# A two-layer hybrid transformer trunk on one core: weight pieces in other buffers, and each engine's order set by a list scheduler inside the kernel

## The chip, the core and the metric

The kernel runs on one core of a Trainium2 chip. The core has five instruction streams that matter here: TensorE (PE, matrix products; PEld is its weight load), VectorE (DVE), ScalarE (ACT), GpSimd (POOL) and SyncE (SP), which issues every DMA of this kernel. Each stream runs its instructions in the order in which they stand in the program; between streams, semaphores say when a result may be used. The metric is the device time of one execution in microseconds (us); lower is better.

## The reference

The input x is 512 tokens by 1024 features, all float32. Two layers, each with a mixing half and a feed-forward half, then a last norm:

```python
mod = jax.nn.silu(c) @ ada_w + ada_b            # six vectors of 1024
h = rms_norm(x, norm_mix) * (1 + sc_m) + sh_m
(aq, ak, av, bq, bkc, bvc, bks, bvs, bkw, bvw, bg, cqkv, cz, ca, cb) = jnp.split(h @ w_in, points, axis=-1)
o_a = banded_attention(rope(aq), rope(ak), av, window=128, sinks)        # 4 heads, 128-token band
o_b = nsa_mixer(bq, bkc, bvc, bks, bvs, bkw, bvw, bg, ...)               # compressed + selected + window
o_c = gated_delta_net(cqkv, ca, cb, cz, conv_w, A_log, dt_bias, norm_w)  # chunked delta rule, 4 heads of 128
x = x + gt_m * (jnp.concatenate([o_a, o_b, o_c], axis=-1) @ w_out)
h = rms_norm(x, norm_ffn) * (1 + sc_f) + sh_f
gate, up = jnp.split(h @ w_gate_up, 2, axis=-1)
x = x + gt_f * ((jax.nn.silu(gate) * up) @ w_down)
```

Inside `nsa_mixer`, `compress_tokens` maps overlapping blocks of 32 tokens through a two-layer network (`silu(flat @ w1) @ w2`), for keys and for values; `w1` is 2048 by 256 for each. Inside `gated_delta_net`, a unit lower triangular matrix per chunk and head is inverted, and a state of 128 by 128 per head is carried from chunk to chunk.

## The kernel before

All activations are kept transposed (features on partitions, 512 tokens along the free axis). A product with a weight is done as three matmuls on float32r: each weight tile `wraw` from DMA is split into a high part `whi` (ACT copies it, L584) and a low part `wlo` (DVE subtracts, L585; sometimes POOL), and `product` multiplies high by high, high by low and low by high. A full-width product of this kind takes 24 matmuls of 128x512.

The mixing half (`layer`) runs, in the order in which it is written: the values of all branches (`pvt`); the delta rule's projections with their short convolutions (`pj`, `convs`); its decays and chunk matrices (`pgr`, `pbr`, `pkk`); the inversion of the chunk matrices, which is a series of small products `pi` on TensorE with a copy by DVE or ACT after each (`prio("inv")`), begun by a substitution on POOL in the tile `lane`; the walk over four chunks (`prio("chain")`: `pks`, `pvn`, `pqs`, `psu`, `pin`, and `pot` for the output); the projections for the two attention branches (`single`, `pair`, with `rope`); the compression (`squeeze`, four pieces of `w1`, products `pcmp`); the attention itself (`attend`: scores `psc`, the mask and row maximum on DVE, exp on ACT, scaling on DVE and POOL, transposes `ppt`, values `poa`, `pob`); and the product with `w_out` in two parts (`pwc` for the delta rule's rows, `pw` for the attention's). The feed-forward half runs over six groups of columns (`pg`, `pu`, then `pd`; from the fifth tile of layer 1 with a seven-product scheme, `pm`). During layer 0 a side stream (`ada`) computes modulation vectors from `ada_w` through the tiles `araw`, on ACT, POOL and DVE.

Weights come through a ring of two buffers, tag `wraw` in pool `wr`, 1 MB each. Each DMA into it waits on SP until the split of the tile two places before is done, and every later DMA stands behind it in SP's queue. The four compression pieces (`craw`, 1 MB each) pass through the same ring, as do the keys of the banded branch (`AK`, 512 KB). Three buffers of 512 KB, tags `ab0` to `ab2`, hold `aq`, `bq` and `bqr` from their projection on; in layer 0 before that the side stream's `araw2` takes turns in them.

What sets the order: the instructions are recorded as the program is written, and the tile framework then orders each engine's stream by its own simulated timeline, shifted by priorities that the kernel gives (`prio`, from the tables `BASE` and `KS`, one table per half layer).

## Time and profile before

| | |
|---|---|
| median of 3 runs | 1449.24 us (1446.93 to 1449.49) |
| profiled execution, its own time | 1450.83 us |
| its span, first to last instruction | 1449.1 us |
| mean granted TensorE clock | 0.968 of full |
| PE, DVE, ACT, POOL busy | 1363.4, 975.1, 685.9, 496.9 us |

The span is 1.7 us short of the execution's own time. Busy time of PE is the union of its matmuls' spans, whose ends are modelled; a gap in it is a stretch in which no matmul was under way. The granted clock is given for each stretch as a mean over time: TensorE ran either at full speed (2.4 GHz) or at half (1.2 GHz), so a mean of 0.83 over a stretch says that it had half the clock in 34% of it.

### The profile page before, as it was taken

The page shows a single profiled execution, that of the slowest core. Times are in us where ns is not written, and L with a number is a line of the kernel's source. Part 1 is how long each engine was busy: PE and PEld are TensorE (multiplying, and loading weights), DVE is VectorE, ACT ScalarE, POOL GpSimd, SP SyncE. Part 2 cuts the span into 40 slices and gives each one's busy share as a digit, 9 for nine tenths or more (in the row PEclk, how much of TensorE's full clock was granted, in tenths as well). Part 3 has the DMA queues.
Part 4 walks back from the last instruction along what each step waited for, and adds up shares of the span by engine and source line. Part 5 has one row for each costly group of instructions (what it writes and reads, how often), then busy time and mean ns, then how long its engine had stood idle before and what let it go on. Part 6 is the DMA issues. An engine that isn't in the chain of part 4 may idle for free.

```text
span 1449.1 us, 22839 instructions
## 1 busy us (share of the span) xinstructions
PE 1363.4 (94%) x8925; PEld 1166.2 (80%) x8925; DVE 975.1 (67%) x1773; ACT 685.9 (47%) x1250; POOL 496.9 (34%) x402
## 2 busy tenths in 40 slices
PE   3889988999999999999999999989989999999997
PEld 2667866877887888788898888667879999898997
DVE  6766886885646555456456667589647787777775
ACT  4576635574543432342245462568544444353441
POOL 4446541254432320140033013224335444253330
PEclk7799999799999999999999999989999999999999
DMA  9647453002147564555441123400130323323322
GB/s 325 208 159 231 142 173 124 29 2 88 30 146 244 162 204 140 166 174 174 133 146 34 59 88 103 153 30 2 43 104 16 121 97 99 106 94 110 117 88 74
DMA packets 137169, 171.57 MB, mean 118 GB/s; under 512 B 14779, under 2 KB 95333, under 8 KB 136933
## 3 DMA queue, kind: packets, MB, share of 16 engines
q1 hardware_dynamic: 137060, 170.11, 36.3%
q8 instruction: 70, 1.15, 0.3%
q14 instruction: 39, 0.31, 0.1%
HBM read 168.00 MB, written 2.10 MB: 117 GB/s over the span
## 4 chain that ended last, share of the span: by engine, by line
PE 66%; DVE 12%; DMA 7%; ACT 5%; POOL 4%; issue 4%; SPq 0%; POOLq 0%; DVEq 0%; ACTq 0%
PE pd L301 16%; PE pm L301 10%; PE pj L301 7%; PE pg L301 7%; PE pu L301 7%; DMA araw<-in_ada_w_dram 5%; PE pw L301 3%; PE psc L301 2%; DVE wlo L585 2%; POOL araw L421 2%; PE pwc L301 2%; PE ppt L1111 2%; PE pob L301 1%; PE pvt L301 1%; DVE araw L416 1%
## 5 line engine op out<-in xcount | busy, mean ns | idle before, releaser
L584 ACT ACTIVATE whi<-wraw 128x1024 fp32r<-128x1024 f32 (+1 forms) x181 | 179.3, 993 | 303.0 <-PE pd L301 99.2
L585 DVE TENSOR_TENSOR wlo<-wraw,whi 128x1024 fp32r<-128x1024 f32 (+1 forms) x171 | 218.5, 1279 | 107.1 <-ACT whi L584 104.9
L301 PE MATMUL pj<-hh,whi 128*128 128x512 f32 (+1 forms) x376 | 149.8, 400 | 7.1 <-DVE cacc L719 3.6
L301 PE MATMUL pj<-hl,whi 128*128 128x512 f32 (+1 forms) x376 | 147.9, 394 | 1.0 <-DVE hl L500 1.0
L301 PE MATMUL pj<-hh,wlo 128*128 128x512 f32 (+1 forms) x376 | 148.0, 394 | 0.8 <-DVE wlo L585 0.8
L421 POOL TENSOR_TENSOR araw<-araw 128x512 f32<-128x512 f32 x55 | 76.7, 1394 | 164.0 <-DMA araw<-in_ada_w_dram 62.8
L599 DVE SCALAR_TENSOR_TENSOR x<-pd,mods,x 128x512 f32<-128x512 f32 (+1 forms) x112 | 73.3, 671 | 65.2 <-PE pd L301 64.0
L301 PE MATMUL pd<-fl,whi 128*128 128x512 f32 x288 | 112.2, 390 | 0.0
L301 PE MATMUL pd<-fh,whi 128*128 128x512 f32 x288 | 111.1, 390 | 1.2 <-ACT whi L584 1.2
L301 PE MATMUL pd<-fh,wlo 128*128 128x512 f32 x288 | 107.3, 390 | 0.0
L301 PE MATMUL pm<-tmix,whi 128*128 128x256 f32 x576 | 102.8, 283 | 0.0
L301 PEld LDWEIGHTS pj<-hh,whi 128*128 128x128 f32 x376 | 72.6, 194 | 24.8 <-issue 5.5
L301 PEld LDWEIGHTS pm<-tmix,whi 128*128 128x128 f32 x576 | 88.2, 192 | 0.0
L301 PEld LDWEIGHTS pj<-hh,wlo 128*128 128x128 f32 x376 | 72.8, 194 | 16.6 <-DVE wlo L585 2.1
L301 PEld LDWEIGHTS pj<-hl,whi 128*128 128x128 f32 x376 | 73.1, 194 | 14.6 <-DVE hl L500 1.2
L301 PE MATMUL pg<-hh,whi 128*128 128x512 f32 (+1 forms) x208 | 78.2, 376 | 3.9 <-ACT hh L496 2.1
L301 PE MATMUL pg<-hh,wlo 128*128 128x512 f32 (+1 forms) x208 | 78.6, 378 | 2.2 <-DVE wlo L585 2.2
L301 PE MATMUL pu<-hh,wlo 128*128 128x512 f32 (+1 forms) x208 | 78.7, 378 | 1.8 <-DVE wlo L585 1.8
L421 POOL TENSOR_TENSOR araw<-araw,araw 128x512 f32<-128x512 f32 x36 | 51.3, 1426 | 81.5 <-ACT araw L420 80.3
L420 ACT ACTIVATE araw<-araw,scol 128x512 f32<-128x512 f32 x91 | 60.6, 715 | 39.1 <-DMA araw<-in_ada_w_dram 37.9
L301 PE MATMUL pg<-hl,whi 128*128 128x512 f32 (+1 forms) x208 | 78.0, 375 | 0.6 <-DVE hl L500 0.6
L301 PE MATMUL pu<-hl,whi 128*128 128x512 f32 (+1 forms) x208 | 77.9, 375 | 0.0
(383 smaller groups left out, 3646.0 us busy)
## 6 DMA issues: line engine op xcount, KB each, us to landing
wraw<-in_w_gate_up_dram SPq DMA_DIRECT2D x44, 1024.0 KB, 5.3
araw<-in_ada_w_dram SPq DMA_DIRECT2D x80, 512.0 KB, 3.9
wraw<-in_w_in_dram SPq DMA_DIRECT2D x22, 1024.0 KB, 5.1
wraw<-in_w_down_dram SPq DMA_DIRECT2D x20, 1024.0 KB, 5.3
araw<-in_ada_w_dram SPq DMA_DIRECT2D x8, 1024.0 KB, 8.3
wraw<-in_w_out_dram SPq DMA_DIRECT2D x8, 1024.0 KB, 5.1
craw<-in_cmp_k_w_dram SPq DMA_DIRECT2D x8, 512.0 KB, 4.0
craw<-in_cmp_v_w_dram SPq DMA_DIRECT2D x8, 512.0 KB, 4.9
```

Source lines behind the costliest of these rows:

```text
L301: return T.matmul(o, l, r, start=start, stop=stop)
L416: V.scalar_tensor_tensor(o, t, scol[:, k:k + 1], acc, op0=OP.mult, op1=OP.add)
L420: A.activation(t, t, AF.Copy, scale=scol[:, k:k + 1])
L421: G.tensor_tensor(o, t, acc, op=OP.add)
L584: A.activation(hi, src, AF.Copy)
L585: eng.tensor_tensor(lo, src, hi.bitcast(F32), op=OP.subtract)
L599: V.scalar_tensor_tensor(xt[m][:, sl], p[:, sl], g, xt[m][:, sl], op0=OP.mult, op1=OP.add)
L1111: T.transpose(p[:, (o + kb) * 128:(o + kb) * 128 + 128], pt[:, kb * 128:kb * 128 + 128], ident)
```

## The change

Two edits. The first moves loads. Pieces 0 and 2 of the compression's `w1` no longer pass through the ring `wraw` but through `ab1` and `ab2`, which wait for `bq` and `bqr`; those two are now taken just before the projection that writes them. The keys of the banded branch are loaded into the second half of the tile `raw2` that already held those of the window and selected branches, so one tile of the ring serves both.

The second edit sets the order. After the program is recorded, a new class `Order` lists all instructions of the five streams, derives from their operands which must follow which, gives each a cost in ns (`_cost`), and builds orders by list scheduling: `backward` ranks each instruction by how much work follows it, `forward` fills the engines by that rank, with a cost for a change of TensorE's tile shape, for ACT's function tables, for outstanding DMAs, and with a rule for TensorE's clock. After up to four turns the order with the shortest result is kept, and every instruction is tied to the one ahead of it on its engine. The computation, the number of products, transposes, vector operations and DMAs are as before. The program's count of ACT table loads goes from 23 to 15, and the number of places in TensorE's order where the tile shape changes goes from 208 to 231.

```diff
+ 'cab': (0, 2),
...
-        aq, bq, bqr = (AB(n, (128, 2, 512), tag=t) for n, t in zip(("aq", "bq", "bqr"), AB3))
+        aq = AB("aq", (128, 2, 512), tag="ab0")
...
-                raw = wr.tile([128, 2, 4, 256], F32, tag="wraw", name="craw")
+                if piece in KN["cab"]:
+                    raw = [AB("craw", tag=t).rearrange("p (a b) -> p a b", a=4) for t in AB3[1:]]
+                else:
+                    t = wr.tile([128, 2, 4, 256], F32, tag="wraw", name="craw")
+                    raw = [t[:, 0], t[:, 1]]
                 for j, n in ((0, "cmp_k_w1"), (1, "cmp_v_w1")):
-                    nc.sync.dma_start(raw[:, j], I[n][l, 512 * piece:512 * piece + 512].rearrange("(i p) c -> p i c", p=128))
+                    nc.sync.dma_start(raw[j], I[n][l, 512 * piece:512 * piece + 512].rearrange("(i p) c -> p i c", p=128))
...
-                        T.matmul(pc[32 * i:32 * i + 32, 256 * j:256 * j + 256], xw[:, j, i], raw[:, j, i],
+                        T.matmul(pc[32 * i:32 * i + 32, 256 * j:256 * j + 256], xw[:, j, i], raw[j][:, i],
...
-        raw2 = wr.tile([128, 2048], F32, tag="wraw", name="wraw")[:, :1024].rearrange("p (k c) -> p k c", k=8)
+        raw2 = wr.tile([128, 2048], F32, tag="wraw", name="wraw").rearrange("p (k c) -> p k c", k=8)
         V.tensor_copy(raw2[:, :, 0:64], raw[:, :, 128:192])
         nc.sync.dma_start(raw2[:, :, 64:128], w_in[:, BKW:BKW + 64].rearrange("(k p) c -> p k c", p=128))
-        single(raw2, lambda p: rope(p, ksw))
+        nc.sync.dma_start(raw2[:, :, 128:256], w_in[:, AK:AK + 128].rearrange("(k p) c -> p k c", p=128))
+        single(raw2[:, :, 0:128], lambda p: rope(p, ksw))
 
         squeeze(0)
-        single(raw_piece(w_in, 0, NK, AK, 128), rope_k)
+        single(raw2[:, :, 128:256], rope_k)
...
+        bq, bqr = (AB(n, (128, 2, 512), tag=t) for n, t in zip(("bq", "bqr"), AB3[1:]))
         pair(BQ, both)
...
+HOP, SWITCH, TABLE, LAND = 70., 95., 1280., 2300.
...
+def _cost(q, i, src, out):
...
+    if q == "S":
+        row = 4 * out.ap[-1][1]
+        size = 4 * n * out.ap[0][1]
+        return 450., size / (385. * (1. if row >= 1024 else max(.25, min(1., row / 600.))))
+    if q == "T":
+        r, c = i.tile_size
+        if "is_transpose=True" in i.concise():
+            o = 107. if r == 128 else 150.
+        elif "float32r" in str(src[0].dtype):
+            o = max(120., .4427 * n)
...
+        return o, o + 165.
+    if q == "A":
+        o = (60. if psum else 120.) + .824 * n + 90. * (len(src) > 1) + 100. * (len(i.outs) > 1)
+        return o, o + 105.
+    if q == "V":
+        o = max(100., 60. + 1.06 * m) + 65. * (len(src) > 2)
...
+class Order:
+    def __init__(self, tc, nc):
+        self.tc = tc
+        work = [i for i in nc.cur_bb.bb.instructions if str(i.engine) in QUEUES and list(i.outs)]
+        self.work, self.n = work, len(work)
+        self.q, self.occ, self.lat, self.table, self.form, self.load, self.sb = [], [], [], [], [], [], []
...
+    def forward(self, rank):
...
+        for _ in range(self.n):
+            t, q = min((max(free[q], 0. if now[q] else later[q][0][0]), q) for q in "STAVG" if now[q] or later[q])
+            while later[q] and later[q][0][0] <= t:
+                x = heapq.heappop(later[q])[1]
+                heapq.heappush(now[q], (-rank[x], x))
+            x = heapq.heappop(now[q])[1]
+            if q == "A" and self.table[x] and self.table[x] != table:
+                other = [p for p in now[q] if self.table[p[1]] in ("", table)]
+                if other:
+                    heapq.heappush(now[q], (-rank[x], x))
+                    x = min(other)[1]
+                    now[q].remove((-rank[x], x))
+                    heapq.heapify(now[q])
+            s, o, l = max(t, ready[x]), self.occ[x], self.lat[x]
+            if q == "A" and self.table[x] and self.table[x] != table:
+                s, table = s + TABLE, self.table[x]
+            if q == "T":
+                if form not in (None, self.form[x]):
+                    s = max(s, free[q] + SWITCH)
+                form = self.form[x]
...
+            if self.sb[x] and pool[0] < s + l and pool[1] > s:
+                b = .5 * (min(s + l, pool[1]) - max(s, pool[0]))
+                o, l = o + b, l + b
+            start[x], free[q] = s, s + o
+            line[q].append(x)
+            if q == "G":
...
+                r = s if not kind else done + HOP if self.q[y] != q or q == "S" else s + (l + 30. if kind == 2 else o)
+                ready[y] = max(ready[y], r)
+                todo[y] -= 1
+                if not todo[y]:
+                    heapq.heappush(later[self.q[y]], (ready[y], y))
+        return max(s + l for s, l in zip(start, self.lat)), start, line
+
+    def backward(self, rank):
...
+            end[x] = free[q] = max(t, ready[x]) + (self.occ[x] if q != "S" else max(450., self.lat[x]))
+            for y, kind in self.pred[x]:
+                r = end[x]
+                if not kind:
+                    r -= self.occ[y]
+                elif self.q[y] != q or q == "S":
+                    r += HOP + (LAND if self.q[y] == "S" else self.lat[y] - self.occ[y])
+                elif kind == 2:
+                    r += 30. + self.lat[y] - self.occ[y]
+                ready[y] = max(ready[y], r)
...
+    def apply(self, turns=4):
+        best = self.forward([-x for x in range(self.n)])
+        last = best
+        for _ in range(turns):
+            last = self.forward(self.backward(last[1]))
+            if last[0] < best[0]:
+                best = last
+        info = mybir.DependencyInfo(mybir.DependencyClass.NoSync, mybir.DependencyReason.DATA)
+        for line in best[2].values():
+            for x, y in zip(line, line[1:]):
+                self.tc.add_manual_dep(self.work[y], self.work[x].name, info, reason="order")
+        return best
+
...
     out = nc.dram_tensor("out_0_dram", (1, S, D), F32, kind="ExternalOutput").ap()
     with tile.TileContext(nc, schedule_with_timeline_sim=True) as tc, ExitStack() as ctx:
         trunk(ctx, tc, aps, out)
+        o=Order(tc, nc)
+        b=o.apply(); print('MODEL',b[0],o.forward([-x for x in range(o.n)])[0])
     r = run_bass_kernel_spmd(nc, [arrays], core_ids=[0])
     return r.results[0]["out_0_dram"]
```

Three places in the order. First TensorE in layer 0 at the end of the inversion (`pi` 64x64, then the first chunk of the walk: `pt`, `pvn`, `psu`, `pin`). Before, the rows between are the banded branch's scores:

```order
L301 MATMUL psc<-akd,aq 128x128 x2
L301 MATMUL pi_1868<-lane,at 64x64 x8
L301 MATMUL pi_1879<-lane,at 64x64 x8
L301 MATMUL psc<-akd,aq 128x128
L301 MATMUL psc<-akd,aq 128x256
L301 MATMUL pi_1890<-up,p_1877 64x64 x8
L301 MATMUL pi_1900<-up,p_1888 64x64 x8
L301 MATMUL psc<-akd,aq 128x128
L301 MATMUL psc<-akd,aq 128x256
L758 MATMUL pt<-cst,ck 128x128 x4
L301 MATMUL pvn<-cv,up 128x128 x4
```

After, they are projections (`pj`, one matmul of 128x512 each):

```order
L304 MATMUL pi_1868<-lane,at 64x64 x8
L304 MATMUL pi_1879<-lane,at 64x64 x8
L304 MATMUL pj<-hh_276,whi 128x512
L304 MATMUL pi_1890<-up,p_1877 64x64 x8
L304 MATMUL pi_1900<-up,p_1888 64x64 x8
L304 MATMUL pj<-hl_277,whi 128x512
L304 MATMUL pj<-hh_276,wlo 128x512
L304 MATMUL pj<-hh_276,whi 128x512
L761 MATMUL pt<-cst,ck 128x128 x4
L304 MATMUL pvn<-cv,up 128x128 x4
L304 MATMUL pj<-hl_277,whi 128x512
L304 MATMUL pj<-hh_276,wlo 128x512
```

The scores left this stretch; one to five projection matmuls stand in each place where a copy by DVE or ACT has to come between two products of the chain.

Second, TensorE in layer 0 during the attention. Before, the walk over the chunks (`pqs`, `psu`, `pin`) stands between the scores and transposes of the attention:

```order
L301 MATMUL psc<-akd,aq 128x256 x2
L301 MATMUL pvn<-cv,up 128x128 x4
L301 MATMUL pqs<-st,cq 128x128 x4
L301 MATMUL psc<-akd,aq 128x256 x2
L301 MATMUL psu<-vn,kd 128x128 x4
L1111 MATMUL ppt<-cst,sc 128x128 x4
L301 MATMUL pcs<-kc,bq 128x64 x2
L301 MATMUL pin<-vn,qk 128x128 x4
```

After, single matmuls of the output product `pwc`, which needs the walk's result, stand between the attention's rows:

```order
L304 MATMUL poa<-ptt,vtok 64x128 x4
L304 MATMUL pwc<-och,wlo 128x512
L1120 MATMUL ppt<-cst,cs_101 128x128
L304 MATMUL pwc<-och,whi 128x512
L304 MATMUL pwc<-ocl,whi 128x512
L304 MATMUL pwc<-och,wlo 128x512
L304 MATMUL pwc<-och,whi 128x512
L304 MATMUL pcs<-kc,bq 128x64 x2
L304 MATMUL pwc<-ocl,whi 128x512
L304 MATMUL pob<-ptt,vcb 128x128 x2
L304 MATMUL pwc<-och,wlo 128x512
L1120 MATMUL ppt<-cst,sc 128x128 x4
```

In layer 0 the walk's last product now stands ahead of the first score; `pwc`, which stood in five long blocks among the last scores and transposes, is spread through the whole attention.

Third, SP's queue in layer 1, from the tiles of the delta rule's projections on (`wraw` 128x8x256 is one; 128x8x64 and 128x8x128 are the window branch's and the banded branch's keys). Before:

```order
L1064 DMA wraw<-in_w_in_dram 128x8x64
L1048 DMA craw<-in_cmp_k_w_dram 128x4x256
L1048 DMA craw<-in_cmp_v_w_dram 128x4x256
L573 DMA wraw<-in_w_in_dram 128x8x128
L1048 DMA craw<-in_cmp_k_w_dram 128x4x256
L1048 DMA craw<-in_cmp_v_w_dram 128x4x256
L573 DMA wraw<-in_w_in_dram 128x8x256
L1048 DMA craw<-in_cmp_k_w_dram 128x4x256
L1048 DMA craw<-in_cmp_v_w_dram 128x4x256
L1048 DMA craw<-in_cmp_k_w_dram 128x4x256
L1048 DMA craw<-in_cmp_v_w_dram 128x4x256
L573 DMA wraw<-in_w_in_dram 128x8x256
```

After, in the same stretch of the queue:

```order
L1055 DMA craw<-in_cmp_v_w_dram 128x4x256
L576 DMA wraw<-in_w_in_dram 128x8x256
L1055 DMA craw<-in_cmp_k_w_dram 128x4x256
L576 DMA wraw<-in_w_in_dram 128x8x256 x4
L843 DMA lane<-consts_dram 128x256
L576 DMA wraw<-in_w_in_dram 128x8x256 x2
L1071 DMA wraw<-in_w_in_dram 128x8x64
L1072 DMA wraw<-in_w_in_dram 128x8x128
L1055 DMA craw<-in_cmp_k_w_dram 128x4x256
L1055 DMA craw<-in_cmp_v_w_dram 128x4x256
L576 DMA wraw<-in_w_in_dram 128x8x256
L1055 DMA craw<-in_cmp_k_w_dram 128x4x256
```

Piece 0 of the compression (the first `craw` pair) stands far ahead, among the projections' tiles; the keys' load stands directly behind the tile that it shares; piece 2 no longer waits for the ring.

## Rows read from the trace of the kernel before

**Rows 1.** The page, part 1: busy us, share of the span, instructions.

```profile
span 1449.1 us, 22839 instructions
...
PE 1363.4 (94%) x8925; PEld 1166.2 (80%) x8925; DVE 975.1 (67%) x1773; ACT 685.9 (47%) x1250; POOL 496.9 (34%) x402
```

**Rows 2.** Busy time by stretch (columns as printed; PEclk: granted clock, 1.00 full).

```profile
core 0: us, PE busy (x) PEld busy (x) DVE busy (x) ACT busy (x) POOL busy (x), PEclk, DMA share, GB/s
0.00:57.00 57.00, 25.84 (x100) 20.41 (x101) 43.22 (x58) 25.85 (x43) 22.69 (x25) 0.67 0.94 313
57.00:150.00 93.00, 84.58 (x413) 69.90 (x412) 59.80 (x94) 65.54 (x101) 54.99 (x41) 0.94 0.52 168
150.00:387.00 237.00, 223.24 (x1825) 180.01 (x1823) 176.43 (x444) 130.63 (x302) 95.83 (x90) 0.95 0.29 89
200.00:268.00 68.00, 57.41 (x711) 42.85 (x704) 47.57 (x87) 32.14 (x56) 22.05 (x33) 0.83 0.37 120
247.00:342.00 95.00, 88.05 (x648) 71.52 (x647) 77.18 (x275) 61.31 (x183) 38.45 (x33) 0.91 0.04 13
396.00:765.00 369.00, 363.45 (x1776) 305.29 (x1775) 201.53 (x259) 135.44 (x192) 78.32 (x60) 1.00 0.52 166
765.00:1083.00 318.00, 303.00 (x2295) 250.24 (x2293) 218.52 (x529) 174.21 (x375) 94.45 (x93) 0.98 0.22 70
900.00:960.00 60.00, 54.98 (x734) 41.47 (x733) 41.40 (x77) 33.73 (x54) 18.12 (x28) 0.91 0.41 135
```

**Rows 3.** The waits of PE: releaser, us in total, times, longest us.

```profile
PE psc L301 <- DVE mx L1133: 9.1, 9, 5.7
...
PE pj L301 <- ACT whi L584: 2.8, 2, 2.6
```

**Rows 4.** Timeline, layer 0, 249 to 258 us: start us, us, engine, line.

```profile
249.77 3.44 DVE L1000 TENSOR_TENSOR bqs<-bqr,bqs 64x512 fp32r<-64x512 f32 x2
...
253.59 0.79 PE L301 MATMUL psc<-akd,aq 64*128 64x128 f32 x2 [5.70 <-DVE mx L1133]
...
254.40 3.64 PE L301 MATMUL pi<-lane,at 64*64 64x64 f32 x32
```

**Rows 5.** Timeline of SP's queue, layer 0, compression's loads.

```profile
203.33 0.37 SPq L573 DMA_DIRECT2D wraw<-in_w_in_dram  x1
209.37 0.37 SPq L1048 DMA_DIRECT2D craw<-in_cmp_k_w_dram  x1
...
215.53 0.37 SPq L1048 DMA_DIRECT2D craw<-in_cmp_k_w_dram  x1
```

**Rows 6.** Chain that ended last, one piece: start us, us, what.

```profile
861.77 5.46 PE pj L301 x24
```

**Rows 7.** Timeline of PE at a change of tile shape.

```profile
289.89 0.73 PE L301 MATMUL psc<-bks,bqs 128*128 128x512 f32 x2
290.56 0.66 PE L301 MATMUL poa<-ptt,vtok 128*64 128x128 f32 x8
```

**Rows 8.** Groups by line, ACT, table loads: busy us, mean ns.

```profile
L721 ACT ACT_TABLE_LOAD x5 | 6.4, 1283 | 13.3 <-DVE cacc L719 13.2
```

**Rows 9.** Groups by line, DVE, 247 to 342 us: the delta rule's.

```profile
L978 DVE SCALAR_TENSOR_TENSOR cq<-pin,gcols,cq 128x128 f32<-128x128 f32 x12 | 3.4, 338 | 0.0
L945 DVE SCALAR_TENSOR_TENSOR cv<-pks,gcols,cv 128x128 f32<-128x128 f32 x12 | 3.3, 337 | 0.0
...
L923 DVE SCALAR_TENSOR_TENSOR osq<-pot,vcol,cz 128x512 f32<-128x512 f32 x4 | 3.0, 741 | 0.0
L925 DVE TENSOR_TENSOR ocl<-osq,och 128x512 fp32r<-128x512 f32 x4 | 2.7, 679 | 0.0
L763 DVE TENSOR_REDUCE so<-osq 128x4 f32<-128x512 f32 x4 | 2.7, 673 | 0.0
L970 DVE SCALAR_TENSOR_TENSOR st<-st,eg,psu 128x128 f32<-128x128 f32 x8 | 2.2, 338 | 0.0
L937 DVE TENSOR_TENSOR kd<-pt,gcols 128x512 f32<-128x512 f32 x3 | 2.1, 686 | 0.4 <-PE pt L758 0.4
```

More of the change, by code (lines that the diff above doesn't have):

```diff
@@ L1 @@
 from contextlib import ExitStack, contextmanager, nullcontext
+import heapq
 import numpy as np
@@ L1522, in trunk, with _span @@
             ffn(l, iter(()), norm, Last, last)
+HOP, SWITCH, TABLE, LAND = 70., 95., 1280., 2300.
+QUEUES = {"EngineType.SP": "S", "EngineType.PE": "T", "EngineType.DVE": "V", "EngineType.Activation": "A",
+          "EngineType.Pool": "G"}
+def _span(ap):
+    return int(np.prod([n for _, n in ap.ap[1:]]))
+def _cost(q, i, src, out):
+    n = _span(out)
+    m = max([n] + [_span(a) for a in src])
+    psum = any("PSUM" in str(a.bass_ap.tensor.space) for a in src if a.bass_ap.tensor.space is not None)
+    kind = type(i).__name__
+    if q == "S":
[8 more added lines that the diff above has]
+            o = max(120., .4427 * n)
+        elif r == 32:
+            o = 19.
+        elif (r, c) == (64, 64):
+            o = 117.
+        else:
+            o = max(35. if c == 32 else 145., 1.74 * n * c / 128)
+        return o, o + 165.
[4 more added lines that the diff above has]
+        o = max(100., 60. + 1.06 * m) + 65. * (len(src) > 2)
+        if kind == "InstReciprocal":
+            o = 200. + 4.7 * n
+        elif kind == "InstStreamTranspose":
+            o = 100. + 1.6 * n
+        return o, o + 85.
+    if kind == "InstMemset":
+        o = 50. + .85 * n
+    elif "pow" in str(getattr(i, "op", "")):
+        o = 480. + 150. * n
+    elif kind == "InstTensorScalarPtr":
+        o = 230. + 2.85 * n
+    else:
+        o = 120. + 3.1 * n if n < (250 if len(out.ap) > 2 else 130) else 140. + 2.2 * n
+    return o, o + 40.
```

115 lines of the change are left out of this document (added).

## The prediction

> **What bounds the kernel now.** I read the page first. PE is busy for 1363.4 of 1449.1 us, the other engines for half to two thirds [rows 1]: the kernel is bound by TensorE's work, and no order can take away more than the time in which TensorE stands still or runs at half its clock. So I then asked for the stretches. In each, idle time is the length less PE's busy time, and the time lost to the clock is at most the length times one less the granted clock, since half the speed loses half the time [rows 2]:
>
> - 0 to 57 us, until the first products run densely: idle 31.2, clock 0.67, so at most 18.8 more.
> - 57 to 150 us: idle 8.4, clock 0.94, 5.6 more: 14.0.
> - 150 to 387 us, the rest of layer 0's mixing: idle 13.8, clock 0.95, 11.9 more: 25.6. Of this the 68 us from 200 to 268 hold 10.6 and, at a clock of 0.83, 11.6: 22.2.
> - 396 to 765 us, layer 0's feed-forward half: idle 5.6 at full clock.
> - 765 to 1083 us, layer 1's mixing: idle 15.0, clock 0.98, 6.4 more: 21.4. Of this the 60 us from 900 to 960 hold 5.0 and 5.4: 10.4.
>
> Behind the start, some 67 us are there to be had, and half of them sit in two short stretches at the same place of both layers: compression and inversion. The start is set by what must be loaded first, and layer 1's feed-forward half has next to nothing.
>
> The timeline shows what goes wrong there in layer 0 [rows 4]. At 249.77 DVE stands for 3.44 us on two instructions that prepare the selected branch's queries, with the score of the banded branch behind them. TensorE has put out two scores, wants a third buffer, and stands for 5.70 us until DVE has read one; that is the longest of nine such waits, 9.1 us in all [rows 3]. Its next products, the 32 small ones of the inversion, then take 3.64 us at the lower clock [rows 4]. In the same stretch SP issues the ring's loads 6.0 and 6.2 us apart, 203.33, 209.37, 215.53 [rows 5], each waiting for a split; TensorE waits 2.6 us for such a split [rows 3].
>
> **The change part by part.** The sum is made against the profiled execution, 1450.8 us, which is 1.6 above the median.
>
> *The order at the inversion, layer 0.* The scores leave the stretch; the chain's products get projections between them, each 5.46 / 24 = 0.23 us [rows 6]. From the first product of the inversion to the first of the walk the new order has 33 such matmuls, 7.5 us, so the chain's copies are mostly covered, and DVE has no attention work ahead of them. The 5.70 us wait has no cause left. I keep 4 of the 22.2 us, for copies of which one or two matmuls cover only part and for a short spell at half clock: **-18**. Bounds: -22, if nothing is left, and -10, if the clock stays as now and only the idle time goes.
>
> *The same in layer 1:* 10.4 us, of which I keep 3.4: **-7**. Bounds -10.4 and 0.
>
> *The two load edits.* They take three of nine users out of the ring, so the remaining tiles start up to three steps of 6 us earlier [rows 5]. What that was worth is the 2.6 us wait above, which stands in the 22.2 already: **0** on its own. The new buffers add waits. In layer 0 `ab1` and `ab2` are in use by the side stream until just before, and SP's later loads queue behind the first compression load; but over 100 projection matmuls, some 26 us, stand ahead of the first compression product in the new order, more than four of SP's steps. `bq` and `bqr` now wait for piece 2's products, with the last projections' copies behind them on ACT and DVE; those projections come after piece 2 in the order anyway. If this cover is gone, one step of 6 us per layer is the price: bounds 0 and +12.
>
> *The rest of both mixing halves:* 14.0 + 3.4 + 11.0 = 28.4 us of scattered waits of 0.3 to 3 us. A new order removes some and makes others. I take a third: **-9.5**. Bounds: 0 and -14, a half.
>
> *Layer 0's feed-forward half:* 5.6 us in waits of about 1 us, where a transposed piece of the side stream cuts into a product. The new order puts those pieces between products: **-1.5**. Bounds 0 and -4.
>
> *The start:* TensorE's first 50 instructions stand as before, and so do the first ten loads: **0**, bounds -3 and +3.
>
> *Tile shapes.* 23 more changes of shape. Two score matmuls of 512 columns between two rows of another shape take 290.56 - 289.89 = 0.67 us [rows 7], against 2 x 0.23 undisturbed [rows 6]: about 0.1 us for each change, **+2.3**. Bounds 0 and +5. The Trainium skill says in "TensorEngine Tiling (Array Packing)", Key Properties, that a change of tiling mode drains TensorE, which speaks against an order that makes more of them; no figure stands there, and the trace's 0.1 us prices the drain as small.
>
> *Table loads.* Eight fewer on ACT at 1283 ns [rows 8] are 10.3 us of an engine that is busy 47% of the time [rows 1]. TensorE's work covers them, **0**; bound -3, if a few stood on the path. The Trainium skill ("ScalarE: Activation LUTs", What ACT_TABLE_LOAD costs) has the same 1283 ns and adds a drain of about 1380 ns to each, which would free some 21 us of ACT; no row here shows that part, and the sum would still be 0.
>
> *The attention.* Now from 247 to 342 us, with the walk inside: DVE 77.2, ACT 61.3 [rows 2]. The walk takes its seven DVE groups along, 3.4 + 3.3 + 3.0 + 2.7 + 2.7 + 2.2 + 2.1 = 19.4 us [rows 9], so DVE keeps 57.8 and ACT less than 61.3. With three engines near 60 in one stretch and only `pwc` as filler, 96 matmuls or 22 us, some waits are new: **+3**. Bounds 0 and +14.
>
> Sum: -18 - 7 + 0 - 9.5 - 1.5 + 0 + 2.3 + 0 + 3 = -30.7. So 1450.8 - 30.7 = 1420.1 for the profiled execution, and 1.6 less for a median: 1418.5, which I round to **1419**.
>
> **The rivals.**
>
> *The clock falls anyway.* The new order's stretches of projections between the chain's copies are short, and small products of 32 by 32 fill the rest. If TensorE is granted half its clock there for as long as now, the terms of the two inversions shrink to the idle time less what I keep: 10.6 - 4 and 5.0 - 3.4, so -6.6 and -1.6 in place of -18 and -7, and the time is 1419 + 16.8 = 1436. For it: the clock of 0.83 in rows that hold just this chain [rows 2]. Against it: much of that slow time followed the 5.70 us stop, which goes. The Trainium skill describes this case in "TensorE: Matmul & The Clock Gate", HAM oscillation: a kernel whose bursts of matmuls are separated by waits is throttled again at each of them. Here the bursts would be the one to eight projections between copies.
>
> *The attention stretch does not shrink.* This one is slower than before. Without the walk, each block of scores goes from PE to DVE, ACT, DVE or POOL, PE, ACT and PE in turn, and the walk's matmuls, which hid that chain, now run elsewhere. I counted on about 68 us per layer (ACT's 61.3 and a tenth). If the softmax chain is the limit and the stretch keeps its 95 us, each layer loses 27: 1419 - 3 + 54 = 1470. It decides from a stretch of 85 us on, where 2 x 17 eats up the gain of 33.7. For it: DVE's reading of scores already ended nine of PE's waits [rows 3]. Against it: DVE loses a quarter of its work there, and the order spreads `pwc` through the stretch.
>
> *The waits only move.* The order rests on costs that are not the chip's; if each engine stands as much as now at other places, the time is that of now, 1449. For it: two engines at 80% of a stretch leave little slack. Against it: the largest waits have a named cause that is gone.
>
> *Everything fits:* all terms at their better bounds but the scattered ones, -22 - 10.4 - 14 - 4, and +2.3: 1401.
>
> **How the numbers follow.** The forecast (1408 to 1432) 0.62; the clock (1432 to 1446) 0.12; everything fits (below 1408) 0.10; waits only move 0.04; the attention's chain 0.12. A measurement of this kernel can tell about 0.2% from no change. Faster by more than that: 0.62 + 0.12 + 0.10 = 0.84; within it 0.04; slower 0.12. The range leaves out the attention's case and the better half of the best one: 1400 to 1447.
>
> **What would show it.** Right: no wait of PE over 3 us between the last decay product and the first score in either layer; a clock above 0.93 in the inversion's stretch; the stretch from first to last score near 70 us; eight table loads fewer; SP's compression loads no longer 6 us apart. Wrong: a stretch from first to last score of 85 us or more with PE waiting for DVE or ACT; half clock through the inversion; PE waits for a compression load, which would say that the new buffers come free too late.

## The result, and the profile after

The change makes the kernel slower: 1456.84 us median of five runs (1455.73 to 1459.27) against 1449.49 of five (1446.93 to 1453.24), ratio 1.006, 95% interval 1.0042 to 1.0079. The forecast was 1419, so the sign is wrong. The profiled execution of the changed kernel took 1459.27 us.

The page of the changed kernel, part 1, answers to [rows 1]:

```profile
span 1457.5 us, 22886 instructions
...
PE 1378.6 (95%) x8925; PEld 1164.6 (80%) x8925; DVE 975.6 (67%) x1773; ACT 681.1 (47%) x1242; POOL 499.3 (34%) x402
```

ACT has 1242 instructions in place of 1250, the eight table loads that went. PE stands still for less time in all, 1457.5 - 1378.6 = 78.9 us against 85.7 before; the same 8925 matmuls are under way for 15 us longer. So the time isn't mainly in waits that a list of waits would show.

Busy time by stretch, columns as in [rows 2]: layer 0's mixing of the kernel before,

```profile
41.40:387.10 345.70, 320.88 (x2278) 260.69 (x2276) 251.23 (x556) 203.48 (x413) 153.79 (x132) 0.93 0.37 118
```

and of the changed kernel, the start left out, its four halves (mixing, feed-forward, mixing, feed-forward):

```profile
39.00:390.60 351.60, 323.69 (x2280) 256.95 (x2280) 255.20 (x554) 203.06 (x413) 162.79 (x135) 0.95 0.38 118
390.60:767.70 377.10, 373.48 (x1837) 315.86 (x1838) 210.67 (x280) 144.22 (x211) 87.92 (x69) 0.99 0.51 164
767.70:1090.70 323.00, 312.20 (x2296) 251.27 (x2295) 219.38 (x522) 170.12 (x365) 91.11 (x89) 0.95 0.21 67
1090.70:1457.50 366.80, 356.16 (x2463) 331.40 (x2462) 263.11 (x379) 147.21 (x228) 141.01 (x91) 1.00 0.28 91
```

Layer 0's mixing grew from 345.7 to 351.6 us, layer 1's from 318.0 [rows 2] to 323.0; the feed-forward halves and the start changed by less than 1 and by 2.4 us. The loss sits where the forecast saw the gain. In layer 1 it can be read off: idle time fell from 15.0 to 10.8 us, but the clock from 0.98 to 0.95, which is 6.4 against 16.2 us at most: 9.8 - 4.2 = +5.6, and the half is 5.0 longer. In layer 0 idle time grew by 3.1, the clock gave 6.6 back, and some 9.4 us remain that are neither (a clock is printed to 0.01, which is up to 1.8 us in such a half): products that are under way longer. The stretches inside the two halves of the changed kernel (decay products to first score, its two parts, first to last score; then in layer 1 inversion to first score, first to last score):

```profile
128.70:271.80 143.10, 128.15 (x1154) 104.15 (x1152) 103.03 (x199) 62.89 (x114) 53.13 (x55) 0.92 0.40 123
128.70:195.40 66.70, 57.49 (x314) 46.54 (x312) 57.16 (x103) 28.96 (x51) 41.74 (x46) 0.95 0.59 181
195.40:271.80 76.40, 70.66 (x841) 57.62 (x840) 45.87 (x97) 33.92 (x64) 11.39 (x9) 0.89 0.23 73
271.80:351.60 79.80, 72.53 (x454) 51.30 (x454) 60.55 (x211) 53.97 (x156) 31.99 (x25) 0.96 0.10 35
888.80:967.10 78.30, 76.08 (x873) 61.09 (x873) 44.78 (x90) 39.52 (x71) 12.61 (x12) 0.96 0.28 91
967.10:1052.10 85.00, 80.57 (x491) 57.02 (x491) 66.55 (x231) 57.87 (x163) 26.89 (x21) 0.86 0.08 28
```

First to last score takes 79.8 and 85.0 us, where I counted on 68. The stretch of decay products has become a new place of waiting: VectorE is busy there for 57.16 of 66.70 us and PE is idle for 9.2. The waits of PE by cause, answering to [rows 3] (releaser, us in total, times, longest), show that the wait of 5.7 us went and others, of up to 3.3 us, came:

```profile
PE psc L304 <- DVE mx L1142: 9.3, 10, 2.7
...
PE pi L871 <- issue: 4.7, 2, 3.3
...
PE pt L729 <- ACT cacc L726: 2.5, 1, 2.5
PE pj L304 <- ACT cz L825: 2.4, 1, 2.4
```

The scores wait for VectorE as long as before in the sum, 9.3 against 9.1 us. SP's queue, answering to [rows 5], does in part what the change was to do: the loads of `cmp_k` for two pieces of the compression stand 1.7 us apart where their buffers are free,

```profile
180.09 0.37 SPq L1055 DMA_DIRECT2D craw<-in_cmp_k_w_dram  x1
180.50 0.96 SPq L1055 DMA_DIRECT2D craw<-in_cmp_v_w_dram  x1
181.81 0.37 SPq L1055 DMA_DIRECT2D craw<-in_cmp_k_w_dram  x1
```

and the next two follow at 194.71 and 214.96 us. No wait of PE in the list is for a compression load.

### The profile page after: what moved, and what is told of

Read it like the earlier page. It is cut to its first block, busy times and chain, and to the rows that moved or that the text cites. A ratio compares the mean times of both kernels' runs of the same rounds, so it can differ in the third digit from the quotient of the medians.

```text
span 1457.5 us, 22886 instructions
## 1 busy us (share of the span) xinstructions
PE 1378.6 (95%) x8925; PEld 1164.6 (80%) x8925; DVE 975.6 (67%) x1773; ACT 681.1 (47%) x1242; POOL 499.3 (34%) x402
## 4 chain that ended last, share of the span: by engine, by line
PE 66%; DVE 16%; POOL 6%; ACT 4%; issue 4%; DMA 3%; SPq 0%; DVEq 0%; POOLq 0%; ACTq 0%
PE pd L304 15%; PE pj L304 9%; PE pu L304 8%; PE pg L304 8%; PE pm L304 6%; DVE wlo L588 4%; PE pwc L304 3%; PE pw L304 2%; PE psc L304 2%; DMA araw<-in_ada_w_dram 2%; PE ppt L1120 2%; PE pob L304 2%; DVE araw L419 2%; PE pvt L304 1%; ACT whi L587 1%
## 5 line engine op out<-in xcount | busy, mean ns | idle before, releaser
L588 DVE TENSOR_TENSOR wlo<-wraw,whi 128x1024 fp32r<-128x1024 f32 (+1 forms) x171 | 223.1, 1305 | 93.3 <-ACT whi L587 91.2
L304 PE MATMUL pd<-fh,wlo 128*128 128x512 f32 x288 | 112.6, 392 | 0.0
L304 PEld LDWEIGHTS pj<-hh,whi 128*128 128x128 f32 x376 | 72.5, 193 | 20.5 <-issue 2.9
L1324 POOL TENSOR_TENSOR vtok<-wraw 128x512 f32<-128x512 f32 x18 | 27.6, 1532 | 167.7 <-DVE wlo L588 89.0
L424 POOL TENSOR_TENSOR araw<-araw,araw 128x512 f32<-128x512 f32 x36 | 54.3, 1510 | 85.3 <-ACT araw L423 84.2
L304 PEld LDWEIGHTS pj<-hl,whi 128*128 128x128 f32 x376 | 72.5, 193 | 11.4
L304 PE MATMUL pm<-tmix,wlo 128*128 128x256 f32 x288 | 81.4, 283 | 0.0
L304 PE MATMUL pg<-hh,whi 128*128 128x512 f32 (+1 forms) x208 | 78.9, 379 | 1.9 <-ACT hh L502 1.3
```

What stands on the lines that cost most here:

```text
L304: return T.matmul(o, l, r, start=start, stop=stop)
L424: G.tensor_tensor(o, t, acc, op=OP.add)
L588: eng.tensor_tensor(lo, src, hi.bitcast(F32), op=OP.subtract)
L1324: G.tensor_tensor(v[:, 0], a[1][0], a[1][1], op=OP.add)
```

## The experiments

Three theories were on the table. **A**: the order costs the time, because the attention without the walk has too little to fill it. **B**: the new buffers of the load edits cost a wait. **C**: the order is planned with durations that are not the chip's, so its waits only move. All ratios are to the kernel before, on the same chip and in the same rounds.

**One part alone.** `loads_only` keeps the load edits and drops the order:

```diff
-        o=Order(tc, nc)
-        b=o.apply(); print('MODEL',b[0],o.forward([-x for x in range(o.n)])[0])
```

> The two load edits stay, the list scheduler's order is not applied: the order is that of the framework, as before. Theory A (the loss is in the order: what it gained ahead of the scores is given back in the attention and in the convolution stretch of layer 0): 1449, within 3 us of the kernel before. Theory B (the new buffers cost a wait of one step of SP, 6 us, per layer): 1455 to 1461. The bounds of my own term for the load edits were 0 and +12; if the freed places in the ring were worth something by themselves, 1444 to 1447.

Measured: 1440.83 us, ratio 0.9959 (0.9944 to 0.9975). `order_only` puts the class `Order` on the program of before:

```diff
         trunk(ctx, tc, aps, out)
+        Order(tc, nc).apply()
```

> The list scheduler's order is applied to the program of before, without the two load edits; it makes its own order for that program. Theory A (the order costs the time): 1455 to 1460, as the whole change. Theory B (the new buffers cost it): 1445 to 1450. Theory C (the order is made from costs that are not the chip's, so each such order lands somewhere by accident): any value between 1440 and 1465, and a PE order that differs in many places from that of the whole change at about the same time.

Measured: 1459.92 us, ratio 1.0089 (1.007 to 1.0109). Theory B is out: with the load edits alone the kernel is some 6 us faster, and the order loses 0.9% or 13 us without them and 1.0% or 15 us with them (1.006 against 0.9959). The halves of `loads_only`, in order:

```profile
40.50:378.90 338.40, 316.95 (x2278) 259.32 (x2276) 249.83 (x556) 204.50 (x412) 154.90 (x132) 0.94 0.39 122
378.90:760.20 381.30, 374.28 (x1836) 315.32 (x1837) 208.58 (x276) 141.65 (x207) 82.34 (x66) 0.99 0.50 162
760.20:1076.20 316.00, 303.65 (x2296) 251.82 (x2295) 215.41 (x529) 174.78 (x375) 93.51 (x94) 0.97 0.22 69
1076.20:1443.60 367.40, 355.33 (x2462) 332.66 (x2462) 269.30 (x377) 147.90 (x226) 145.62 (x90) 0.99 0.27 91
```

Against this, the order lengthens the mixing by 13.2 and 7.0 us and shortens layer 0's feed-forward half by 4.2. (The profiled execution of `loads_only` took 1445.4 us, 4.6 above its median, so stretches compared with it are uncertain by that much.) The framework makes its order anew for the changed program, so the 6 us can be the freed ring or another order; no run separates them.

**Part of the ties.** `att_free` ties all but the attention's instructions, `pe_ties` only TensorE's; in both the framework places the rest.

```diff
         for line in best[2].values():
+            line = [x for x in line if not any(a <= x < b for a, b in zip(MARK[::2], MARK[1::2]))]  # att_free
+            line = [x for x in line if self.q[x] == 'T']                                            # pe_ties
```

> The whole change, but the instructions of the attention (scores, softmax, transposes, value products, preparation of the selected branch, of both layers) are left out of the imposed order; the framework places them among the others. Theory A (the loss sits in the attention as the order plays it): first to last score again with other work inside, 1440 to 1450. Theory C (the loss sits in all parts of the order alike): 1453 to 1460. If the imposed order of all the other instructions is the harm: above 1460.

> The whole change, but only TensorE's instructions are held to the list scheduler's order; VectorE, ScalarE, GpSimd and the queue of loads get the order of the framework. If the order of TensorE alone makes the time (the longer busy time of PE, 15 us): 1454 to 1461. If the orders of VectorE and ScalarE are at fault (instructions that stand ahead of those which PE waits for): 1440 to 1450. If the framework fits the other engines badly to this PE order, above 1462.

Measured: 1473.54 us (1.0181, 1.0155 to 1.0207) and 1531.47 us (1.0584, 1.056 to 1.0608). Both are worse than the whole. So the framework doesn't repair an order that it gets for one engine or around a hole; neither run tells which engine's order is at fault, and `att_free` can't be used for or against A.

**The walk back inside the attention, and dearer durations.** `walk_in` adds to the list scheduler's graph that chunk c of the walk comes behind the first score of block c. `cost_fit` raises the planned durations: the code plans VectorE's subtraction of 1024 columns at 60 + 1.06 x 1024 = 1145 ns, while the group in the changed kernel's trace (busy us, mean ns) shows

```profile
L588 DVE TENSOR_TENSOR wlo<-wraw,whi 128x1024 fp32r<-128x1024 f32 x145 | 205.3, 1416 | 91.2 <-ACT whi L587 89.2
```

`hop150` raises the time from one engine to the next; `walk_fit`, `hop_fit` and `hop_fit_walk` combine them.

```diff
+        for y, x in zip(SCORE, WALK):                 # walk_in
+            self.succ[y].append((x, 0))
+            self.pred[x].append((y, 0))
+        o *= 1.165   # cost_fit: ACT;  VectorE 1.2, GpSimd 1.157
-HOP, SWITCH, TABLE, LAND = 70., 95., 1280., 2300.
+HOP, SWITCH, TABLE, LAND = 150., 95., 1280., 2300.   # hop150
```

> The whole change, with one rule more in the list scheduler: the first product of the walk's chunk c may not be issued before the first score of the banded branch's block c, so the walk lies inside the attention again, as before the change. Theory A (the attention lost its filler: 80 and 85 us for some 53 and 56 us of products, at half clock for 23.9 us in layer 1): the stretch ahead of the scores gets shorter by what the walk took there, the half clock in layer 1's attention goes, and the time is 1440 to 1449. Theory C (the order is planned with durations that are too short, so the waits only move): 1452 to 1462, with the waits of the attention now ahead of the scores.

> The whole change, with the list scheduler's durations raised to what the trace of the changed kernel shows in the sum: VectorE by 1.2, ScalarE by 1.165, GpSimd by 1.157. Theory C (VectorE's 1057 us were planned some 170 us too short, so the order puts products where VectorE has not delivered): 1435 to 1449, with less waiting of PE in the stretch of the convolutions and the decay products of layer 0. Theory A: 1453 to 1460, since a better price does not give the attention a filler.

> Both edits, the walk inside the attention and the durations raised. Theory A alone: as walk_in, 1440 to 1449. Theory C alone: as cost_fit, 1435 to 1449. If the two causes are separate and add: 1430 to 1442, that is at or below the kernel with the load edits alone.

> The whole change, with the scheduler's time from one engine to the next raised from 70 to 150 ns, which keeps consumers further behind their producers. Theory C: faster than the change, 1440 to 1452, if short waits of PE for VectorE and ScalarE are what was planned too thin. Theory A: 1453 to 1460. If each order lands by accident, anywhere from 1445 to 1470.

> The whole change with raised durations and 150 ns from engine to engine together. Theory C, durations planned too short: the two edits answer the same fault, so together they give little more than the better one, 1438 to 1444. If each order lands by accident: anywhere from 1440 to 1460, so above the run with 150 ns alone as often as not.

> All three edits: raised durations, 150 ns from engine to engine, the walk inside the attention. If the walk's place is worth the 5 us by which both edits together beat the raised durations alone: 1432 to 1438. If the walk's place is worth nothing, as with the change's own durations: as the run without it, 1438 to 1444. By accident: above 1446.

| run | median us | ratio | 95% interval |
|---|---|---|---|
| walk_in | 1457.03 | 1.0051 | 1.0031 to 1.007 |
| cost_fit | 1451.97 | 1.0029 | 1.0014 to 1.0044 |
| walk_fit | 1446.51 | 0.9983 | 0.9965 to 1.0 |
| hop150 | 1442.93 | 0.9969 | 0.9954 to 0.9984 |
| hop_fit | 1448.12 | 1.0015 | 0.9996 to 1.0033 |
| hop_fit_walk | 1454.77 | 1.0066 | 1.0044 to 1.0088 |

`walk_in` speaks against A. In layer 1 it does what it was made for: the clock of that half rises from 0.95 to 0.98. But idle time there rises from 10.8 to 17.9 us, and the half is as long as in the change. In layer 0's attention (the second line, first to last score) the clock is 0.88 in place of 0.96.

```profile
767.60:1090.49 322.89, 304.95 (x2295) 250.16 (x2293) 217.17 (x521) 167.76 (x363) 90.05 (x88) 0.98 0.21 67
245.24:344.60 99.36, 91.22 (x586) 68.71 (x585) 74.55 (x267) 63.12 (x182) 33.38 (x30) 0.88 0.04 14
```

The three edits don't add up: each of the dearer plans alone is faster than the change, all together is not. That speaks against C as I had put it, a plan with too thin a margin, and for the case named last in three of the expectations: where an order lands is an accident.

**The attention without filler.** `pwc_late` lets no `pwc` be issued ahead of the first score of the full branch's last block:

```diff
+        for k, x in enumerate(WC):
+            y = LAST[7 + 8 * (k // 8)]
+            self.succ[y].append((x, 0))
+            self.pred[x].append((y, 0))
```

> The whole change, but the 96 output products of pwc in each layer may not be issued before the last block's first score of the full branch: the attention has nothing to fill it. If the softmax chain sets the attention's length (my rival, deciding from 85 us on): first to last score stays at 78 to 85 us, the 22 us of pwc come behind, and the time is 1485 to 1500. If pwc is no filler but lengthens the attention by its own time: first to last score shrinks to about 60 us and the time stays within 5 us of 1457. Between the two: what part of pwc was hidden.

Measured: 1453.88 us, ratio 1.0054 (1.0033 to 1.0075), the change's time within the intervals. First to last score of the two layers:

```profile
256.00:327.73 71.73, 67.44 (x447) 47.30 (x446) 55.65 (x223) 53.97 (x165) 24.84 (x23) 0.86 0.06 19
953.80:1029.25 75.45, 67.64 (x447) 47.97 (x447) 60.31 (x228) 54.21 (x165) 22.05 (x20) 0.84 0.04 15
```

71.7 and 75.5 us: taking nearly all of `pwc` out shortens the stretch by 8.1 and 9.5 us only, and it is still longer than the 68 us on which I had counted with 22 us of `pwc` in it. It isn't empty, though. The new order put some 60 small products of the walk and the compression into it (`pvn`, `pqs`, `pin`, `pot`, `pct`, `pkc`, `pvc`), about 10 us per layer by their groups, of which the change has none there in layer 0 and 4.6 us in layer 1. And TensorE is busy for 67.4 and 67.6 us of the two stretches, so they don't show how long the chain of the softmax alone would take. The `pwc` products are also slower among the scores. `pwc`, one of its three groups (busy us, mean ns), in the change:

```profile
L304 PE MATMUL pwc<-och,whi 128*128 128x512 f32 x64 | 28.1, 439 | 0.0
```

(in layer 0's attention alone, at a clock of 0.96, it is 437 ns) and in `pwc_late`:

```profile
L311 PE MATMUL pwc<-och,whi 128*128 128x512 f32 x64 | 25.3, 395 | 0.0
```

From the first score to the first product of the feed-forward half, 256.0 to 382.5 and 953.8 to 1085.1, `pwc_late` is nearly 8 us longer per layer than the change (126.5 and 131.3 us against 118.8 and 123.6), but it also holds the small products just named, so how much of `pwc` the scores cover can't be read off. The total stayed, because the stretch from the decay products to the first score, which the edit doesn't touch, came out at 127.3 us in layer 0, 15.8 shorter.

**Is an order a draw?** Three runs differ from the change in one number, 60, 75 and 100 ns in place of 70.

> The whole change with 60 in place of 70 ns from engine to engine. If the margin between engines is what counts (150 ns gave 14 us): slightly slower than the change, 1457 to 1462. If each order is a draw: anywhere from 1440 to 1470, with no trend over 60, 70, 75, 100, 150.

> The whole change with 75 in place of 70 ns. If the margin counts: 1455 to 1457. If each order is a draw: anywhere from 1440 to 1470.

> The whole change with 100 in place of 70 ns. If the margin counts: between the change and the run with 150, 1448 to 1454. If each order is a draw: anywhere from 1440 to 1470.

| ns from engine to engine | 60 | 70 (the change) | 75 | 100 | 150 |
|---|---|---|---|---|---|
| median us | 1444.51 | 1456.84 | 1448.53 | 1444.52 | 1442.93 |
| ratio | 0.998 | 1.006 | 1.0001 | 0.9987 | 0.9969 |
| 95% interval | 0.9963 to 0.9997 | 1.0042 to 1.0079 | 0.9986 to 1.0016 | 0.997 to 1.0005 | 0.9954 to 0.9984 |

The runs show no trend from 60 to 100: the change's own number is the worst of the five, and a step of 10 ns down gives as much as one of 30 up. Where the five part is layer 0, decay products to first score; `hop60` (this stretch, then first to last score):

```profile
130.45:255.80 125.35, 117.20 (x1117) 95.01 (x1115) 99.40 (x189) 60.52 (x110) 52.34 (x55) 0.99 0.44 139
255.80:340.36 84.56, 77.63 (x481) 54.19 (x481) 63.16 (x226) 55.41 (x161) 30.72 (x25) 0.90 0.09 28
```

and `hop100`, this stretch alone:

```profile
130.69:259.75 129.06, 118.31 (x1122) 96.47 (x1120) 98.13 (x190) 61.50 (x111) 54.87 (x55) 0.97 0.44 135
```

125 and 129 us at a clock of 0.99 and 0.97, against the change's 143.1 at 0.92. The 17.8 us between the change and `hop60` are waits and clock nearly whole: 14.9 + 11.4 us in the one, 8.2 + 1.3 in the other. Some 8 us of it are a single stop in the inversion and the half clock behind it (last section). The attention is no shorter in `hop60`, 84.6 us.

**One half alone.** `ffn_fit`, `ffn_ties` and `ffn_hop100` tie only the instructions of the two feed-forward halves, with 150 ns and raised durations, with the change's numbers, and with 100 ns; `mix_ties` ties only the mixing halves, with the change's numbers.

```diff
         for line in best[2].values():
+            line = [x for x in line if any(a <= x < b for a, b in zip(MARK[1::2], MARK[2::2] + [self.n]))]
```

> The load edits stay, and only the instructions of the two feed-forward halves are held to the list scheduler's order, made with raised durations (VectorE 1.2, ScalarE 1.165, GpSimd 1.157) and 150 ns from engine to engine; both mixing halves keep the framework's order. By parts of the runs so far: mixing as with the load edits alone (338 and 316 us), feed-forward halves as in the runs with raised numbers (370 to 371 and 362 to 365, against 381 and 367): some 13 us below the load edits alone, 1425 to 1435. If the order of one half can't be joined to the framework's of the other without new waits at the seams: 1438 to 1450. If the list scheduler is worth nothing in any half: 1441.

> The load edits, and only the instructions of the two mixing halves held to the list scheduler's order, with the change's own durations; the feed-forward halves are the framework's. If the mixing halves carry the loss: mixing 350 and 322 us as in the change, feed-forward 381 and 367 as with the load edits alone, 1455 to 1466. If the loss came from the whole (seams between the halves, state that one half leaves to the next): 1440 to 1450.

> The load edits, and only the feed-forward halves held to the list scheduler's order, with the change's own durations and 70 ns. If the order of the feed-forward halves is worth something whatever the planning numbers: 1429 to 1438. If the gain was a draw: as the load edits alone or anywhere from 1436 to 1455.

> The load edits, and only the feed-forward halves held to the list scheduler's order, with the change's own durations and 100 ns. If the order of the feed-forward halves is worth something whatever the planning numbers: 1429 to 1438. If the gain was a draw: 1436 to 1455.

| run | median us | ratio | 95% interval |
|---|---|---|---|
| mix_ties | 1473.11 | 1.0159 | 1.0112 to 1.0205 |
| ffn_fit | 1433.15 | 0.9921 | 0.9899 to 0.9943 |
| ffn_ties | 1435.65 | 0.992 | 0.9906 to 0.9935 |
| ffn_hop100 | 1434.29 | 0.9908 | 0.9891 to 0.9924 |

With only the feed-forward halves tied the kernel beats both others, and here three orders agree. The halves of `ffn_hop100`:

```profile
40.43:376.89 336.46, 313.18 (x2279) 256.52 (x2277) 249.70 (x556) 204.20 (x412) 154.89 (x132) 0.95 0.39 122
376.89:755.38 378.49, 373.50 (x1836) 316.23 (x1837) 209.92 (x280) 143.84 (x211) 86.85 (x70) 0.99 0.51 163
755.38:1066.02 310.64, 300.46 (x2296) 249.42 (x2294) 213.83 (x526) 172.85 (x370) 91.10 (x89) 0.98 0.22 70
1066.02:1432.48 366.46, 356.67 (x2462) 333.00 (x2462) 260.30 (x376) 146.41 (x226) 140.74 (x90) 0.99 0.28 91
```

Against `loads_only` the feed-forward half of layer 0 gains 2.8 us, and layer 1's mixing, whose own instructions are not tied, gains 5.4, about half of the 11.1 us between the two spans. By the ratios, 0.9908 against 0.9959, the distance is some 7 us; the rest is that the profiled run of `loads_only` lies above its median. In `mix_ties` the feed-forward half of layer 0 takes 381.3 us, as with the load edits alone, and the mixing 349.7 and 331.9. It is 1% slower than the whole change, so what the halves cost doesn't add up either.

## Why the prediction was wrong

- **The step that failed is the attention.** The sum took its length from "about 68 us per layer (ACT's 61.3 and a tenth)", with "three engines near 60", and put +3 for new waits; no row for TensorE's own time in it stood behind that. Measured: 79.8 and 85.0 us. Idle time and clock, read as in the prediction, cost at most 7.3 + 3.2 us there in layer 0 and 4.4 + 11.9 in layer 1, 26.8 in all. The kernel before lost 1.2 and 2.7 us, at full clock, from the end of the inversion's stretches to its last scores:

```profile
268.00:341.80 73.80, 72.57 (x552) 59.25 (x552) 60.38 (x233) 50.89 (x161) 34.83 (x30) 1.00 0.01 1
960.00:1037.20 77.20, 74.54 (x551) 59.78 (x551) 62.58 (x241) 52.85 (x170) 33.83 (x29) 1.00 0.01 3
```

So some +23 us in place of +3. The busiest engine of the changed stretches is TensorE, 72.53 and 80.57 us, not ACT with 53.97 and 57.87. Less the waits and the clock, some 69 us are left in each layer (an estimate from these rows), so 68 could not be met even without a wait. The rival "the attention stretch does not shrink" was right that this stretch makes the change slower, at about half its size: 11.8 and 17.0 us over the 68, in place of 27 each. Its mechanism, the softmax chain as the limit, is seen only in part: the scores' waits for VectorE are most of the idle time (6.9 of 7.3 us in layer 0, 2.4 of 4.4 in layer 1), but in layer 1 the half clock costs more than all waits together. This holds beyond the change: `hop60`, 12 us faster, takes 84.6 and 88.2 us from first to last score and loses 6.9 + 8.5 and 5.4 + 12.3 in them. That the change lies above its neighbours is the draw. At the middle ratio of the five, 0.9987, the order would still have given back some 4 of the 6 us that came with the load edits.

- **The order at the inversion**, -18 and -7: right in sign, too large. By the same reading, over stretches that don't hold quite the same work, the changed kernel loses 5.7 + 8.4 = 14.1 us in 195.4 to 271.8 and 2.2 + 3.1 = 5.3 in 888.8 to 967.1, against 22.2 and 10.4. So -8 and -5: the 5.70 us wait went, but a stop of 3.34 us with half clock behind it came, some 8 us of the 14.1. The lower bound of layer 0, -10, had been closer.
- **The scattered waits**, -9.5: about -7.8 outside these stretches. Part of them only moved, to the decay products, where TensorE is idle for 9.2 us in 128.7 to 195.4.
- **"The waits only move"** is what happened to the two mixing halves as a whole: idle time and clock together cost at most 24.8 + 24.2 and 15.0 + 6.4 = 70.4 us before and 27.9 + 17.6 and 10.8 + 16.2 = 72.5 after.

Term by term, from the span of the kernel before to that of the changed one, 1449.1 to 1457.5 us. The third row is not read off: it is what is left of the 10.9 us by which the two mixing halves grew.

| term | forecast | measured, us |
|---|---|---|
| inversion, both layers | -25 | -13.1 |
| attention, new waits and clock | +3 | +22.9 |
| products longer under way (tile shapes in the forecast) | +2.3 | +8.8 |
| other waits and clock of the mixing halves | -9.5 | -7.8 |
| feed-forward halves | -1.5 | -0.1 |
| start | 0 | -2.4 |
| sum (rounded) | -30.7 | +8.4 |

- **Tile shapes**, +2.3: no run takes them alone. What they cost lies in the 8.8 us, with whatever else makes a product longer.
- **The clock falls anyway**: it did, in layer 0's inversion behind the 3.34 us stop, and in layer 1's attention, which I had not thought of.
- **The load edits**, 0: mis-sized. With them alone the kernel is 5.9 us faster (0.41% of 1447.6), outside my bounds of 0 and +12. The wait that I feared, for buffers that come free late, isn't there.
- **Layer 0's feed-forward half**, -1.5: measured -0.8, and -4.2 against `loads_only`, where it takes 381.3 us. The start, 0 within 3: -2.4. **Table loads**, 0: eight went, as foreseen. ACT's busy time fell by 4.8 us, not by the 10.3 of eight loads; what that was worth no run shows.
- **Of the signs that I named**: no wait of PE over 3 us ahead of the scores: missed, one of 3.34; clock above 0.93 in the inversion: no in layer 0 (0.89), yes in layer 1 (0.96); near 70 us of attention: no; SP's compression loads closer: the first two, not the rest; stretch of 85 us with PE waiting for DVE or ACT: the length in layer 1 (85.0), of which 4.4 us are idle time.

What was shown, and what was not. It is shown that the mixing halves carry the loss (`mix_ties` against the three `ffn` runs), that the load edits don't, and that orders planned by one rule with one number a little different lie 0.9% or 13 us apart, the change's being the slowest of five. The change's distance to its neighbours lies in layer 0's stretch ahead of the scores, which is 12 to 18 us longer in it than in the four others. What stays open is why the scores wait and the clock falls in every one of these attentions, and why the framework's order of the mixing, 338 and 316 us, beats all the whole orders, which took 340 to 353 and 316 to 328: neither the walk in the attention nor longer planned durations nor more margin reaches it in both layers.

## What to carry to other kernels

When work is moved out of a stretch, work out the new length from the time of every engine in it, TensorE's own too, each from a row. Then put a price on waits and half clock there as well: here they cost 26.8 us where 3 were allowed. Before judging a scheduler by one order, vary a number that shouldn't matter: if the times lie 1% apart, the order is a draw, and a gain that holds over several draws (here the feed-forward halves alone, 0.992, 0.992 and 0.991) is worth more than the best of them. Cut an all-or-nothing change to its parts; here the change was slower and two of its three parts, kept without the third, are, within the noise, the fastest kernel of the study.

## What the runs showed of the hardware

TensorE got half its clock while its records show it nearly always busy. In the changed kernel, layer 1, around the first scores and then among them:

```profile
962.00:972.60 10.60, 8.88 (x48) 7.08 (x47) 7.68 (x13) 10.30 (x18) 2.52 (x2) 1.00 0.12 45
972.60:996.50 23.90, 22.69 (x71) 12.30 (x71) 19.20 (x70) 14.46 (x46) 11.88 (x10) 0.50 0.13 45
```

PE is idle for only 1.2 of 23.9 us, yet the granted clock is 0.50 throughout; the products are small ones of scores and values with single `pwc` between them. The fall comes 2 us behind a wait of 1.36 us (969.2 to 970.6), the longest in the two rows. So a stretch that looks full can run at half clock: busy time alone doesn't show it. The Trainium skill, "TensorE: Matmul & The Clock Gate", A second HAM failure mode, describes a kernel whose short pauses between groups of matmuls make the clock go back and forth between its two levels; the trace agrees only in part. The waits in this stretch are short, but there are two of them, 0.43 and 0.63 us, and the clock stays down. No run here separates the pauses from the kind of product.

In the run of 128 small products of the inversion PE stopped for 3.34 us with nothing in the profile to wait for (start us, us, engine, line):

```profile
198.02 0.64 PE L871 MATMUL pi<-pq,td 32*32 32x32 f32 x50
202.00 1.29 PE L871 MATMUL pi<-pq,td 32*32 32x32 f32 x78 [3.34 <-issue]
```

The clock fell within this stop and stayed at half for some 9 us behind it, with PE busy all the time:

```profile
201.20:211.30 10.10, 9.30 (x156) 7.46 (x156) 4.62 (x8) 0.59 (x1) 0.00 (x0) 0.50 0.01 3
```

Before the change no such stop stands in the inversion, nor in `loads_only`, `ffn_ties` and `ffn_hop100`. Every kernel whose mixing halves follow the list scheduler, whole or in part, has at least one; the longest of each is between 0.7 and 3.3 us (`ffn_fit` has one of 0.4). The cause wasn't tried. One candidate can be named: from 194 to 206 us two DMA queues named "instruction" carried packets (packets, MB, share), one packet of each queue within the stop.

```profile
q8 instruction: 2, 0.03, 1.4%
q14 instruction: 1, 0.01, 0.2%
```
